# Window-attention scores: the low-part product over all 128 rows instead of over 64

## The chip, the cores and the metric

The kernel runs on one core of a Trainium2 chip. The metric is the device time of one execution in microseconds. Three timed runs of the kernel before gave 893.3, 894.34 and 895.06 us; the median is 894.34 us.

## The reference

One layer of a hybrid decoder over 512 tokens of 1024 channels: a norm, three token mixers side by side (chunked linear attention with 4 heads, a short gated convolution, sliding-window attention), their gated sum, an output projection, a second norm and a gated MLP with 2816 channels and a convolution of width 3. All in float32.

The change lies in the sliding-window attention. It has 8 query heads, 2 key heads and 64 channels per head. The tokens stand in four blocks of 128; a query sees the keys of its own block up to itself and those of the block before that are less than 128 tokens away:

```python
    qb = (q.astype(f32) * hd ** -0.5).reshape(Bsz, Nb, W, Hkv, G, hd)
    kw = windows(k)                       # 256 keys: the block before and its own
    scores = jnp.einsum('bnqhgd,bnkhd->bnhgqk', qb, kw)
    logits = jnp.where(valid[None, :, None, None], scores + alibi, -jnp.inf)
    m = jnp.maximum(logits.max(axis=-1), sink)
    p = jnp.exp(logits - m[..., None])
    denom = p.sum(axis=-1) + jnp.exp(sink - m)
    o = jnp.einsum('bnhgqk,bnkhd->bnqhgd', p, vw) / jnp.moveaxis(denom, 4, 2)[..., None]
```

## The kernel before, in words

Float32 accuracy is made of products in float32r: each factor is split into a high part (its rounding) and a low part (the rest), and a product is high x high + high x low + low x high, without low x low.

The weights come as a stream of blocks of 2048 columns per partition (class W, lines 52 to 101): SyncE loads a block, ScalarE writes its high part (line 91), VectorE its low part (line 92), a block or more ahead of the products that use it. The large products take most of the time: by_channel (line 171; its products all stand on line 177) and by_token (lines 183 to 186). Every 12 products by_channel calls tick, which advances the tasks in the list `side` by one step each. Linear attention and window attention run as such side tasks beside the large products.

The window attention's queries come from four tiles of 128 channels (lines 595 to 602), each of which holds two heads in its lower and upper 64 rows. For each head there is a tile sq with the query's high part in the head's own 64 rows and its low part in the other 64 rows. The keys are stored for either of the 2 key heads as skh (high part) and skl (low part), each of them twice, in the lower and in the upper 64 rows (lines 605 to 609). So a product over all 128 rows of sq and skh gives high x high + low x high in one instruction, and one over the 64 rows that hold the query's high part, with skl, adds high x low.

window(n) handles one block of 128 queries. Its steps, one at each tick: the scores of four heads (scores(0)), then those of the other four (scores(1)) while the first are evicted by ScalarE (line 655), masked (line 656), given their bias and reduced to a maximum by VectorE (line 660); the exponentials on ScalarE (line 680); the division on VectorE (line 686); eight transposes on TensorE (line 693); their eviction with a mask on VectorE (line 698); the products with the values on TensorE (line 706), and the split of the result (lines 709 and 710). A window starts five steps behind the one before. The order in which the instructions of an engine are put down is not that of the Python text alone: a planner with a simulated timeline (line 988) may move them.

The stationary operand of each score product is the block of 128 queries, and 256 keys of skh or skl move past it. Each product has its own weight load (PEld in the profile), also where two in a row have the same stationary operand. One call of scores gives eight products into two banks of PSUM; four windows with two calls each give 64.

Of the kernel before, what the change touches and what calls it, by code (L numbers as in the profile page):

```python
# [23 lines left out]
EPS = 1e-6  # L24
TAU = 16.0
NCONST = 6 * P
NSLOT = 45  # scratch tiles of [128, 512] up to the output projection
HEAD_STEPS = 3  # steps from the start of one linear-attention head to that of the next
LAG_STEPS = 5  # steps that a head's products wait for their factors
WINDOW_STEPS = 5  # steps from one window's start to the next one's  # L30

GQ, GK, GV, GR, GA = 0, 512, 1024, 1536, 2048
CX, CB, CC = 2064, 2576, 3088
# [4 lines left out]
def trunk(ctx, tc, x, g_mix, w_in, w_alpha, b_alpha, norm_g, conv_w, sinks, w_gla, w_conv, w_swa,  # L38
# [11 lines left out]
        return ps.tile([P, 512], F32, tag="b", name="bank")  # L50

    class W:
        """A stream of weight blocks of 2048 columns per partition, each split exactly into two
        float32r parts. While the products of block i run, block i + 1 is split, in pieces, and
        block i + 2 is loaded."""

        def __init__(self):
            self.todo, self.raw, self.done, self.pieces = [], [], [], []
# [45 lines left out]
    at = {}  # L104
    side = []

    def tick():
        """One step of whatever runs beside the large products."""
        w.piece()
        for task in list(side):  # L110
            if next(task, side) is side:
                side.remove(task)
# [78 lines left out]
        nc.vector.tensor_sub(out=lo, in0=src, in1=hi.bitcast(F32))  # L191

    def rstd_of(ss, n, tag, log=False):
        """(ss / n + EPS) ** -0.5, refined by one Newton step."""
        shape = list(ss.shape)
        v = small.tile(shape, F32, tag=tag + "v", name="v")
        r = small.tile(shape, F32, tag=tag + "r", name="r")
        t = small.tile(shape, F32, tag=tag + "t", name="t")
        nc.vector.tensor_scalar(out=v, in0=ss, scalar1=1.0 / n, scalar2=EPS, op0=ALU.mult, op1=ALU.add)
        if log:  # L200
            nc.scalar.activation(out=t, in_=v, func=AF.Ln)
            nc.scalar.activation(out=r, in_=t, func=AF.Exp, scale=-0.5)
        else:
            nc.scalar.activation(out=t, in_=v, func=AF.Sqrt)
            nc.vector.reciprocal(out=r, in_=t)
        u = small.tile(shape, F32, tag=tag + "u", name="u")
        nc.vector.tensor_mul(out=u, in0=r, in1=r)
        nc.vector.tensor_mul(out=u, in0=u, in1=v)
        nc.vector.tensor_scalar(out=u, in0=u, scalar1=-0.5, scalar2=1.5, op0=ALU.mult, op1=ALU.add)
        nc.vector.tensor_mul(out=r, in0=r, in1=u)  # L210
        return r

    def rstd_1(ss, e, n, tag, log=False):
        """(ss / n + e[0]) ** -0.5 for one column, refined by one Newton step; e[1] is -e[0] / 2."""
        v = small.tile([P, 1], F32, tag=tag + "v", name="v")
        r = small.tile([P, 1], F32, tag=tag + "r", name="r")
        t = small.tile([P, 1], F32, tag=tag + "t", name="t")
        if log:
            nc.scalar.activation(out=t, in_=ss, func=AF.Ln, scale=1.0 / n, bias=e[0])
            rstd_1.last = nc.scalar.activation(out=r, in_=t, func=AF.Exp, scale=-0.5)  # L220
        else:
            nc.scalar.activation(out=t, in_=ss, func=AF.Sqrt, scale=1.0 / n, bias=e[0])
            nc.vector.reciprocal(out=r, in_=t)
        nc.vector.tensor_scalar(out=v, in0=ss, scalar1=-0.5 / n, scalar2=e[1], op0=ALU.mult, op1=ALU.add)
        nc.vector.tensor_scalar(out=v, in0=v, scalar1=r, scalar2=r, op0=ALU.mult, op1=ALU.mult)
        nc.vector.tensor_scalar(out=r, in0=v, scalar1=1.5, scalar2=r, op0=ALU.add, op1=ALU.mult)
        return r

    def rstd_part(ss, n, tag, engine=nc.vector):
        """The first part of a sum of squares, for rstd_1 of the rest."""  # L230
        e = small.tile([P, 2], F32, tag=tag + "e", name="e")
        engine.tensor_scalar(out=e[:, 0:1], in0=ss, scalar1=1.0 / n, scalar2=EPS, op0=ALU.mult, op1=ALU.add)
        engine.tensor_scalar_mul(e[:, 1:2], e[:, 0:1], -0.5)
        return e[:, 0:1], e[:, 1:2]

    # ---- the input and its norm
    zero = pc.tile([P, 256], F32, name="zero")
    nc.vector.memset(zero, 0.0)
    idle = bank()

    def warm(n):
        """Products of zeros, to hold the tensor engine's clock up until the input is there."""
        for _ in range(n):
            mm(idle[:, 0:256], zero[:, 0:P], zero, start=True, stop=True)

# [78 lines left out]
        return ul[:, k, :]  # L324

    def a_tile(name, j, n=slice(0, S), acc=None):
        """Tile j of the channels of a weight block, by token."""
        if name == "gq0":
            hi, lo = (a.rearrange("p (j k c) -> p j k c", j=2, c=P)[:, j] for a in w.take(at[name]))
        else:  # L330
            hi, lo = (a.rearrange("p (k j c) -> p j k c", j=2, c=P)[:, j] for a in w.take(at[name]))
        acc = acc or bank()
        by_channel(acc, lambda k: hi[:, k], lambda k: lo[:, k], uhk, ulk, n=n)
        return acc

    def b_tiles(name):
        """The four token tiles of 512 channels, each as it is ready."""
        accs = [bank() for _ in range(NT)]
        for i in range(2):
            hi, lo = (a.rearrange("p (k c) -> p k c", c=512) for a in w.take(at[f"{name}{i}"]))  # L340
            for t in range(NT):
                tok = slice(t * P, (t + 1) * P)
                by_token(accs[t], lambda k: uh[:, 4 * i + k, tok], lambda k: ul[:, 4 * i + k, tok],
                         lambda k: hi[:, k, :], lambda k: lo[:, k, :], 4, i == 0, i == 1)
                if i:
                    yield t, accs[t]

    # ---- linear attention: queries, keys and gates
    qs, ks = [None] * GH, [None] * GH

    def got_q(h, acc):
# [78 lines left out]
            la[h] = z  # L430

    def running_sums(y, n):
        """In place: the sums of the first 1, 2, .. n of every n columns."""
        s = 1
        while s < n:
            g = y.rearrange("p (g s) -> p g s", s=2 * s)
            nc.vector.tensor_add(out=g[:, :, 2 * s - 1], in0=g[:, :, 2 * s - 1], in1=g[:, :, s - 1])  # L437
            s *= 2
        s = n // 4
        while s:  # L440
            g = y.rearrange("p (n g s) -> p n g s", s=2 * s, g=n // (2 * s))
            nc.vector.tensor_add(out=g[:, :, 1:, s - 1], in0=g[:, :, 1:, s - 1], in1=g[:, :, :-1, 2 * s - 1])
            s //= 2

    # ---- linear attention: the factors of each head
    ATs, qIs, kTs, decs = [None] * GH, [None] * GH, [None] * GH, [None] * GH

    def factors(h):
# [89 lines left out]
        nc.scalar.copy(out=v, in_=acc)  # L538
        vs.append(v)

    # ---- linear attention: states and outputs
    Os = [None] * NT

    def normed(n, O):
# [44 lines left out]

    side.append(states())  # L590

    # ---- window attention
    lower, upper = slice(0, 64), slice(64, 128)
    sqs = []
    for t in range(4):
# [36 lines left out]
    def window(n):  # L632
# [6 lines left out]
        def scores(pr):  # L639
            sps = [bank() for _ in range(2)]  # L640
            for i in range(2):
                for g in range(2):
                    rg = upper if i else lower
                    q = sqs[4 * g + 2 * pr + i]
                    s_ = sps[i][:, 256 * g:256 * g + 256]
                    mm(s_, q[:, c], skh[g][:, kc], start=True, stop=False)  # L646
                    mm(s_, q[rg, c], skl[g][rg, kc], start=False, stop=True)  # L647
            return sps

        def biased(pr, sps):  # L650
            """Each query's last 128 keys: those of its own block up to itself, the others of the block before."""
            for i in range(2):
                s = slot(name="sc")[:, 0:256].rearrange("p (g j) -> p g j", g=2)
                ps2 = sps[i].rearrange("p (g j) -> p g j", g=2)
# [63 lines left out]
    side.append(values())  # L718
    side.append(windows())

    # ---- short convolution
    def conv3(acc, cwj, name):
        """Three causal taps over the tokens, from PSUM or SBUF."""
        y = slot2(name=name)
        nc.scalar.activation(out=y, in_=acc, func=AF.Copy, scale=cw[:, 2, cwj:cwj + 1])  # L725
        nc.vector.scalar_tensor_tensor(out=y[:, 1:], in0=acc[:, :S - 1], scalar=cw[:, 1, cwj:cwj + 1],  # L726
# [24 lines left out]
            och.append(hi)  # L751
            ocl.append(lo)

    # ---- linear attention: output gate
    ogh = [slot(F32R, name="ogh") for _ in range(4)]
    ogl = [slot(F32R, name="ogl") for _ in range(4)]

# [15 lines left out]
    for t, acc in b_tiles("gr"):  # L773
        side.append(gated(t, acc))

    # ---- the gated sum of the branches
    mh, ml = [], []
    for j in range(4):
        gts = []
# [29 lines left out]
    uh = pU.tile([P, KT, S], F32R, name="uh2")  # L809
    ul = pU.tile([P, KT, S], F32R, name="ul2")  # L810

    # ---- output projection, residual, norm
    gf = [slot(name="gf") for _ in range(2)]
    for i in range(2):
        nc.gpsimd.dma_start(out=gf[i], in_=g_ffn[None, 512 * i:512 * i + 512].to_broadcast([P, 512]))
# [47 lines left out]
                elif two:  # L863
                    h_split(t - 2, hn[t - 2])

    # ---- gated MLP with a convolution
    first3 = [("ug0", 0), ("ug0", 1), ("uu0", 0)]
    early = []
    for i, (name, j) in enumerate(first3):
# [19 lines left out]
    xs = [None] * len(DOWN)  # L889

    def split_prods(i):
        """The factors of block i, split a tile at each step."""
        k0, kt = DOWN[i]
        xs[i] = [[], []]
        for k in range(kt):
            for part, name in zip(xs[i], ("xh", "xl")):
                part.append(pF.tile([P, 512], F32R, tag="t", name=name, bufs=22))
            split(xs[i][0][k], xs[i][1][k], prods[k0 + k])
            yield
# [92 lines left out]
```

## Time and profile before

| | |
|---|---|
| median of 3 timed runs | 894.34 us (893.3 to 895.06) |
| span of the profiled execution | 891.6 us |
| median of the timed runs less that span | 2.7 us |
| PE (TensorE products) busy | 879.0 us, 99% |
| PEld (weight loads) busy | 705.9 us, 79% |
| DVE (VectorE) busy | 475.2 us, 53% |
| ACT (ScalarE) busy | 342.8 us, 38% |
| mean granted TensorE clock | 0.996 |

The span is that of one profiled execution, from the first to the last instruction. What lies around it in that execution isn't given by itself; the timed runs stand 2.7 us above the span. Durations of products are pipelined and their ends are modelled, so a product's duration is longer than its distance to the next one. The window scores lie between 147 and 219 us.

### The profile page before, as it was taken

To read this page: it belongs to the slowest core of one execution; us is meant where nothing else is said; L and a number is where in the kernel's file an instruction comes from. 1 tells how busy PE (TensorE), PEld (TensorE's weight loads), DVE (VectorE), ACT (ScalarE), POOL (GpSimd) and SP (SyncE) were. 2 spreads that over 40 slices of the span, in tenths; PEclk is the share of its full clock that TensorE was granted. 3 is DMA by queue.
4 is the path that set the end of the run, shared out by engine and by line. 5 is a ranking of instruction groups with operands and counts; after the bars stand their busy time and mean duration, and the time that the engine had idled before them with its cause. 6 is when DMAs were issued, how large, how long until landed. Compare 5 with 4: busy or idle time off the path is not lost.

```text
span 891.6 us, 10006 instructions
## 1 busy us (share of the span) xinstructions
PE 879.0 (99%) x3976; PEld 705.9 (79%) x3976; DVE 475.2 (53%) x822; ACT 342.8 (38%) x607; POOL 59.1 (7%) x58
## 2 busy tenths in 40 slices
PE   8999999999999999999999999999999999999996
PEld 6887887767678888888888898888888888888885
DVE  5599566765633251526234666555555555743734
ACT  6545543443434132322223444333333333532533
POOL 2027003000000000101010000000000000001100
PEclk9999999999999999999999999999999999999999
DMA  9431331211222333233325134222222223222202
GB/s 278 145 94 48 95 95 48 86 56 48 78 66 71 95 93 115 77 95 96 87 79 165 48 118 139 93 92 93 94 92 93 92 69 113 96 71 95 95 1 94
DMA packets 69862, 82.39 MB, mean 92 GB/s; under 512 B 2875, under 2 KB 58455, under 8 KB 69815
## 3 DMA queue, kind: packets, MB, share of 16 engines
q1 hardware_dynamic: 69511, 80.70, 28.4%
q0 software_dynamic: 304, 1.05, 0.4%
q8 instruction: 31, 0.51, 0.2%
q14 instruction: 16, 0.13, 0.0%
HBM read 79.64 MB, written 2.10 MB: 92 GB/s over the span
## 4 chain that ended last, share of the span: by engine, by line
PE 92%; DVE 4%; ACT 1%; POOL 1%; issue 0%; DMA 0%; ACTq 0%
PE bank L177 64%; PE bank L184 7%; PE bank L183 7%; PE bank L186 7%; PE bank L647 1%; PE bank L706 1%; PE bank L646 1%; DVE wlo L92 1%; POOL d L461 1%; DVE z L437 1%; DVE d L479 0%; PE bank L693 0%; PE bank L566 0%; DMA h<-in_x 0%; ACT xsq L299 0%
## 5 line engine op out<-in xcount | busy, mean ns | idle before, releaser
L177 PE MATMUL bank<-uh,whi 128*128 128x512 f32 (+1 forms) x792 | 302.7, 386 | 1.9 <-ACT uh L315 1.6
L177 PE MATMUL bank<-ul,whi 128*128 128x512 f32 (+1 forms) x792 | 303.1, 386 | 0.2
L92 DVE TENSOR_TENSOR wlo<-raw,whi 128x1024 fp32r<-128x1024 f32 x144 | 176.5, 1259 | 196.1 <-ACT whi L91 113.0
L91 ACT CAST whi<-raw 128x1024 fp32r<-128x1024 f32 x144 | 144.4, 1048 | 174.6 <-PE bank L177 145.8
L177 PE MATMUL bank<-uh,wlo 128*128 128x512 f32 (+1 forms) x792 | 192.8, 384 | 0.0
L177 PEld LDWEIGHTS bank<-uh,whi 128*128 128x128 f32 x792 | 149.4, 189 | 35.5 <-ACT uh L315 2.1
L177 PEld LDWEIGHTS bank<-ul,whi 128*128 128x128 f32 x792 | 149.8, 189 | 33.4 <-issue 0.8
L177 PEld LDWEIGHTS bank<-uh,wlo 128*128 128x128 f32 x792 | 144.0, 188 | 32.3 <-issue 0.8
L184 PE MATMUL bank<-whi,xl 128*128 128x512 f32 x176 | 68.8, 392 | 0.0
L183 PE MATMUL bank<-whi,xh 128*128 128x512 f32 x176 | 67.9, 391 | 0.0
L186 PE MATMUL bank<-wlo,xh 128*128 128x512 f32 x176 | 48.0, 391 | 0.0
L191 DVE TENSOR_TENSOR xl<-p,xh 128x512 fp32r<-128x512 f32 x44 | 30.2, 726 | 26.9 <-ACT xh L190 22.6
L183 PEld LDWEIGHTS bank<-whi,xh 128*128 128x128 f32 x176 | 33.1, 188 | 7.3
L186 PEld LDWEIGHTS bank<-wlo,xh 128*128 128x128 f32 x176 | 33.1, 188 | 7.2
L184 PEld LDWEIGHTS bank<-whi,xl 128*128 128x128 f32 x176 | 33.1, 188 | 7.1
L190 ACT CAST xh<-p 128x512 fp32r<-128x512 f32 x44 | 24.7, 616 | 36.3 <-PE bank L184 36.3
L725 ACT ACTIVATE yg<-bank,cw 128x512 f32<-128x512 f32 x22 | 15.1, 685 | 53.3 <-PE bank L177 53.3
L797 DVE TENSOR_TENSOR g<-bank,g 128x512 f32<-128x512 f32 x24 | 16.5, 689 | 32.0 <-PE bank L177 31.4
L800 POOL TENSOR_TENSOR g<-g 128x512 f32<-128x512 f32 x8 | 13.4, 1673 | 302.7 <-DVE g L797 300.7
L784 ACT ACTIVATE g<-bank 128x512 f32<-128x512 f32 x24 | 14.3, 596 | 48.2 <-PE bank L177 48.1
L907 ACT ACTIVATE yg<-yg 128x512 f32<-128x512 f32 x22 | 13.9, 631 | 47.9 <-DVE yg L728 47.9
L726 DVE SCALAR_TENSOR_TENSOR yu<-bank,cw,yu 128x511 f32<-128x511 f32 x22 | 16.4, 747 | 26.4 <-ACT yu L725 26.4
(211 smaller groups left out, 963.1 us busy)
## 6 DMA issues: line engine op xcount, KB each, us to landing
raw<-in_w_in SPq DMA_DIRECT2D x28, 1024.0 KB, 5.2
raw<-in_w_up SPq DMA_DIRECT2D x22, 1024.0 KB, 5.1
raw<-in_w_down SPq DMA_DIRECT2D x10, 1024.0 KB, 5.0
raw<-in_w_o SPq DMA_DIRECT2D x4, 1024.0 KB, 5.0
h<-in_x SPq DMA_DIRECT2D x4, 512.0 KB, 4.8
raw<-in_w_gla_o SPq DMA_DIRECT2D x4, 512.0 KB, 3.4
raw<-in_w_conv_o SPq DMA_DIRECT2D x4, 512.0 KB, 4.6
raw<-in_w_swa_o SPq DMA_DIRECT2D x8, 256.0 KB, 4.1
```

Of the source, the lines that this page charges most:

```text
L91: nc.scalar.copy(out=hi[:, c], in_=raw[:, c])
L92: nc.vector.tensor_sub(out=lo[:, c], in0=raw[:, c], in1=hi[:, c].bitcast(F32))
L177: mm(acc[:, n], a, b[:, n], start=i == 0, stop=i == len(todo) - 1)
L183: mm(acc, xh(k), hi(k), start=start and k == 0, stop=False)
L184: mm(acc, xl(k), hi(k), start=False, stop=False)
L186: mm(acc, xh(k), lo(k), start=False, stop=stop and k == kt - 1)
L190: nc.scalar.copy(out=hi, in_=src)
L191: nc.vector.tensor_sub(out=lo, in0=src, in1=hi.bitcast(F32))
L725: nc.scalar.activation(out=y, in_=acc, func=AF.Copy, scale=cw[:, 2, cwj:cwj + 1])
L726: nc.vector.scalar_tensor_tensor(out=y[:, 1:], in0=acc[:, :S - 1], scalar=cw[:, 1, cwj:cwj + 1], in1=y[:, 1:], op0=ALU.mult, op1=ALU.add)
L784: nc.scalar.activation(out=g, in_=acc, func=AF.Sigmoid)
L797: nc.vector.tensor_mul(out=g, in0=acc, in1=g)
```

## The change

The second product of each score takes all 128 rows of sq and skl. The rows added hold the query's low part and another copy of the key's low part, so the scores get the term low x low as well. The helper variable for the 64 rows goes. Otherwise only comments and docstrings are taken out of the text.

```diff
             for i in range(2):
                 for g in range(2):
-                    rg = upper if i else lower
                     q = sqs[4 * g + 2 * pr + i]
                     s_ = sps[i][:, 256 * g:256 * g + 256]
                     mm(s_, q[:, c], skh[g][:, kc], start=True, stop=False)
-                    mm(s_, q[rg, c], skl[g][rg, kc], start=False, stop=True)
+                    mm(s_, q[:, c], skl[g][:, kc], start=False, stop=True)
             return sps
```

## Rows read from the trace of the kernel before

**Rows 1.** The page: busy us (share of the span) and count; the chain's shares by engine.
```profile
PE 879.0 (99%) x3976; PEld 705.9 (79%) x3976; DVE 475.2 (53%) x822; ACT 342.8 (38%) x607; POOL 59.1 (7%) x58
...
PE 92%; DVE 4%; ACT 1%; POOL 1%; issue 0%; DMA 0%; ACTq 0%
```

**Rows 2.** Windows: stretch, length, busy PE, PEld, DVE, ACT, POOL, clock, DMA share, GB/s.
```profile
145.00:236.00 91.00, 91.00 (x379) 64.91 (x378) 58.67 (x193) 38.24 (x119) 2.55 (x2) 1.00 0.22 70
```

**Rows 3.** Timeline of PE, second score group: start us, us, engine, line, operation, shapes.
```profile
152.38 0.28 PE L646 MATMUL bank<-skh,sq 128*128 128x256 f32 x1
152.59 0.38 PE L647 MATMUL bank<-skl,sq 64*128 64x256 f32 x1
152.90 0.39 PE L646 MATMUL bank<-skh,sq 128*128 128x256 f32 x1
...
154.78 0.50 PE L177 MATMUL bank<-uh,whi 128*128 128x512 f32 x1
155.11 0.40 PE L177 MATMUL bank<-ul,whi 128*128 128x512 f32 x1
155.34 0.40 PE L177 MATMUL bank<-uh,whi 128*128 128x512 f32 x1
```

**Rows 4.** Timeline of the weight loads of the same group.
```profile
152.15 0.19 PEld L646 LDWEIGHTS bank<-skh,sq 128*128 128x128 f32 x1
152.59 0.18 PEld L647 LDWEIGHTS bank<-skl,sq 64*128 64x128 f32 x1 [0.25 <-issue]
152.90 0.19 PEld L646 LDWEIGHTS bank<-skh,sq 128*128 128x128 f32 x1
```

**Rows 5.** Timeline of PE, the value products of window 1.
```profile
204.47 1.94 PE L706 MATMUL bank<-pt,sv 128*64 128x512 f32 x8
206.34 1.20 PE L177 MATMUL bank<-uh,wlo 128*128 128x512 f32 x4
```

**Rows 6.** Timeline of PE, a product of 96 rows and the next one.
```profile
46.24 0.40 PE L422 MATMUL bank<-gl,wa 96*128 96x512 f32 x1
46.48 0.40 PE L177 MATMUL bank<-uh,whi 128*128 128x512 f32 x1
```

**Rows 7.** By tile, skh and skl: count, duration ns min/median/max, first and last start.
```profile
L646 PEld LDWEIGHTS bank<-skh,sq x32: 186/186/192, 146.9 to 218.1; 128*128 128x128 f32 x32
...
L647 PEld LDWEIGHTS bank<-skl,sq x32: 182/183/183, 147.3 to 218.4; 64*128 64x128 f32 x32
...
L609 DVE TENSOR_TENSOR skl<-bank,skh x4: 683/688/695, 135.1 to 138.4; 64x512 fp32r<-64x512 f32 x4
```

**Rows 8.** Timeline of PE, a projection tile made in halves of 256 columns.
```profile
25.86 0.28 PE L177 MATMUL bank<-uh,whi 128*128 128x256 f32 x1
25.98 0.28 PE L177 MATMUL bank<-ul,whi 128*128 128x256 f32 x1
26.10 1.11 PE L177 MATMUL bank<-uh,wlo 128*128 128x256 f32 x8
27.05 0.28 PE L177 MATMUL bank<-ul,whi 128*128 128x256 f32 x1
```

**Rows 9.** Timeline of PE, the transposes of window 0 and a score group behind them.
```profile
171.33 1.03 PE L693 MATMUL bank<-cst,sc 128*128 128x128 f32 x8
172.12 0.36 PE L646 MATMUL bank<-skh,sq 128*128 128x256 f32 x1
```

**Rows 10.** Timeline of PE, the transposes of window 2, around the last score group.
```profile
215.47 0.71 PE L693 MATMUL bank<-cst,sc 128*128 128x128 f32 x5
...
217.78 0.55 PE L693 MATMUL bank<-cst,sc 128*128 128x128 f32 x3
```

**Rows 11.** Timeline of VectorE: the divisions of windows 0 and 2, and a split.
```profile
162.16 1.66 DVE L686 TENSOR_SCALAR sc<-sc,rs 128x128 f32<-128x128 f32 x8
...
207.63 2.36 DVE L92 TENSOR_TENSOR wlo<-raw,whi 128x1024 fp32r<-128x1024 f32 x2 [7.33 <-PE bank L177]
...
211.21 1.06 DVE L686 TENSOR_SCALAR sc<-sc,rs 128x128 f32<-128x128 f32 x5
```

## The prediction

> **What bounds the kernel now.** I read the page's busy table and the head of the chain of waits first: TensorE is busy 99% of the 891.6 us span and carries 92% of the chain [rows 1]. So a change pays by what it does to TensorE's own sequence, or by a wait that it puts there. Next the stage of the change: between 145 and 236 us, where the window scores lie, PE is busy for all 91.00 us at a granted clock of 1.00 (the level of 2.4 GHz), VectorE for 58.67 and ScalarE for 38.24 [rows 2], so no product waits there on another engine. Last the timeline, because a busy share of 99% hides how far apart the products start. That matters here: a row's duration holds a pipeline that overlaps with the next product (a 512-column product lasts 0.40 us, and the next starts 0.23 behind it), so I count from start to start, never by durations.
>
> One score group, lines 646 and 647, has eight products of 256 columns in turn: 128 rows, 64 rows, 128 rows and so on [rows 3]. The first 64-row product starts 0.21 us behind the 128-row one; each later start is 0.31 behind the last ((154.78 - 152.59) / 7), though the neighbours with twice the columns start 0.23 apart. The first 512-column product behind the group also takes 0.33 to its successor (154.78 to 155.11). The weight-load rows say why [rows 4]: line 646's first load starts at 152.15, 0.23 ahead of its product at 152.38, beside the product before it, and is hidden. The later ones start with the record of their own product (152.59 and 152.59, 152.90 and 152.90): they have waited until the product before was through. Such a product's record holds its load, 0.38 us instead of 0.28.
>
> Is it 64 rows that cost this, or going from 128 to 64 and back? Other small products answer. Line 706's products, whose stationary block has 64 columns, run eight in a row in 1.87 us (204.47 to 206.34), 0.23 each, no more than 512 columns of the full array [rows 5]. Line 422's product of 96 rows has 0.24 to the full product behind it, so it loses nothing [rows 6]. Small operands are not slow in themselves; what costs is going over between the full array and a half, and a score group does that eight times, its exit included.
>
> **The change, part by part.** No instruction is added or removed: the 32 products of line 647 stay, with their 32 loads [rows 7], 256 columns each as before; only their contraction goes from 64 to 128 rows, and with it the last half-array products leave the score groups. The data are there: line 609 writes both halves of skl by 139.1 us (last start 138.4 plus 0.69), and the first product that reads them starts at 147.3 [rows 7].
>
> (a) The step of a 256-column product among full ones. The trace has such a stretch: the first projection tile is made in two halves of 256 columns, with a 128x128 load for each product, pairs of products on one stationary block (25.86 and 25.98), and accumulation in one place, all three as the scores will have them. There ten steps take 27.05 - 25.86 = 1.19 us, 0.119 each [rows 8]. The loads hide, though a load of that shape lasts 186 ns [rows 7].
>
> (b) One group, from its first product to the second 512-column product behind it. Before: 155.11 - 152.38 = 2.73 us. After: 8 x 0.119 + 0.233 (a 512-column step, 155.34 - 155.11) = 1.185. The gain is 1.545 us: 0.09 on the first step, 7 x 0.194 on the next ones, 0.10 on the exit.
>
> (c) There are eight groups: four windows with two each, 32 products on either line [rows 7]. Three begin right behind the transposes of line 693 (the one at 172.12, [rows 9]), where the first step is a little longer; I leave that in on both sides. The last group is broken by three transposes [rows 10], but the change of shape is still there eight times (64 rows to a transpose counts as one). So 8 x 1.545 = 12.4 us.
>
> (d) Load length: a full load lasts 186 ns against 183 [rows 7]. Hidden it costs nothing; with the cover gone, 32 x 3 ns = 0.1 us.
>
> (e) What is late next. TensorE will reach everything behind a group 1.55 us sooner. Its products in the stage that need other engines are the transposes of line 693 (behind the last multiplication of line 686) and the value products of line 706 (behind line 698). The tightest that I found is window 2: line 686 ends at 211.21 + 1.06 = 212.27 [rows 11], the transposes start at 215.47 [rows 10], a margin of 3.2 us. One group lies between the event that set VectorE going (the split of line 92 at 207.63, released by TensorE) and those transposes, so 1.6 us are left. Window 0 has 171.33 - 163.82 = 7.5 [rows 9, 11] and loses one group too. So no stall in the forecast. VectorE's 58.67 us fit into 91.00 - 12.4 = 78.6 us with a share of 0.75. The weight stream takes 0.22 of the DMA engines in the stage [rows 2] and would take 0.25.
>
> (f) Behind the stage nothing depends on when it ended: the rest is the same row of full products, and the gain is carried to the end.
>
> Sum: the profiled span goes from 891.6 to 879.2 us. The median of the timed runs, 894.34, stands 2.7 us above that span (what lies around it); I keep these: 894.34 - 12.4 = 881.9 us.
>
> Bounds of (a), the only new step. From below, transposes with 128 columns start 0.099 apart (171.33 to 172.12 for eight, [rows 9]); a product of twice the columns can't be counted faster, and 64 x 0.02 = 1.3 us more gain gives 880.6. From above, the step stays as it is now and only (d) is added: 894.4. I take 0.119, since that row is the same kind of product in every respect that the trace shows.
>
> A rule that speaks against this: the Trainium skill, "TensorE: Matmul & The Clock Gate", section "The mechanism", says that a weight load overlaps products in flight only when the row groups differ. By it full products could never hide their loads from one another, the change would leave a group's loads exposed, and the time would be that of the first rival. The step in (a) disagrees with it here.
>
> **Rivals.**
> 1. The step stays; the change doesn't do what it says. The exposed load would come from something that the change keeps, such as the swap of the moving operand (skh, then skl) on one stationary block, or loads that can't pass a product on the same rows. Then 894.34 + 0.1 = 894.4. For it: line 646's products are full, and their loads are exposed too. Against it: (a) has both properties and steps at 0.119, and 96 rows lose nothing. 4%.
> 2. TensorE gets ahead of the softmax. The gain is there, but transposes or value products wait, because ScalarE and VectorE work through their steps in a fixed order and a margin of 1.6 us is thin. If the four windows, with 3.1 us of gain each, give back up to half, the time is 882 to 888, say 885. For it: window 2's margin. Against it: PE never waits in the stage today, and window 0 keeps 5.9 us. 11%.
> 3. Slower: the order is written by a planner (line 988), and in the last group it has already put transposes between scores. Priced anew, it could put a window's transposes directly behind its second score group. From that group's end (154.78) to the end of line 686 (162.16 + 1.66 = 163.82) window 0 needs 9.0 us of ScalarE and VectorE [rows 3, 11]; with nothing else in TensorE's queue, four windows would stand 36 us: 894.34 - 12.4 + 36 = 918. It turns the sign from 12.4 / 4 = 3.1 us per window on. Against it: 256 columns stay 256 columns, and 16.5 us of products lie between these points today (154.78 to 171.33). 2%.
>
> **How the numbers follow.** The forecast has 83%; its own range is 880.6 to 883.4 (the bound of (a), and a stall of as much as the tightest margin). With rival 2 the range goes to 886.5; runs of the kernel before spread from 893.3 to 895.1, so I begin at 880.0. About 0.2% (1.8 us) is what a measurement can tell from no change. Faster by more than that: forecast and rival 2, 94%. Within: rival 1, 4%. Slower: 2%.
>
> **What would show it.** Step (a): in the timeline of the changed kernel, starts 0.12 apart in lines 646 and 647, records of 0.28 us, and loads that start with the product before theirs; rival 1 has 0.31 there. Step (b): 1.2 us from a group's first product to the second 512-column one behind it. Step (e): no wait of TensorE on line 686 or 698, and PE busy throughout a stage that is 12 us shorter; rival 2 shows such waits, rival 3 large ones with line 693 close behind line 647. Step (f): from the stage to the end, the same duration as before. The prediction is wrong if the stage shrinks by less than 8 us, or if it shrinks by 12 and the rest grows.

## The result and the profile after

The changed kernel takes 881.05 us (median of 4 runs, 880.52 to 881.93) against 894.0 us of the kernel before (4 runs): a ratio of 0.9857, 95% interval 0.9843 to 0.9871. Forecast were 881.9 us in a range of 880.0 to 886.5. The profiled span is 879.3 us where the sum gave 879.2.

The page's first lines, as [rows 1] showed them for before:

```profile
PE 866.5 (99%) x3976; PEld 701.9 (80%) x3976; DVE 474.8 (54%) x822; ACT 342.5 (39%) x607; POOL 59.0 (7%) x58
...
PE 92%; DVE 4%; ACT 1%; POOL 1%; DMA 1%; issue 0%; SPq 0%; ACTq 0%
```

The counts are the same, PE has lost 12.5 us, and its share and its part of the chain stand where they stood. A kernel that is bound by TensorE at 99% can still have 12 us of air in it, if that air lies inside the records.

The second score group on PE's timeline answers to [rows 3] (lines 646 and 647 of before are 645 and 646 now):

```profile
150.93 0.28 PE L645 MATMUL bank<-skh,sq 128*128 128x256 f32 x1
151.05 0.28 PE L646 MATMUL bank<-skl,sq 128*128 128x256 f32 x1
151.17 0.28 PE L645 MATMUL bank<-skh,sq 128*128 128x256 f32 x1
...
151.88 0.40 PE L177 MATMUL bank<-uh,whi 128*128 128x512 f32 x1
152.11 0.39 PE L177 MATMUL bank<-ul,whi 128*128 128x512 f32 x1
```

From its first product to the second 512-column one the group takes 152.11 - 150.93 = 1.18 us, where it took 2.73. The weight loads of the same group, against [rows 4]:

```profile
150.94 0.19 PEld L646 LDWEIGHTS bank<-skl,sq 128*128 128x128 f32 x1
151.05 0.19 PEld L645 LDWEIGHTS bank<-skh,sq 128*128 128x128 f32 x1
151.17 0.19 PEld L646 LDWEIGHTS bank<-skl,sq 128*128 128x128 f32 x1
```

Line 646's load now starts at 150.94, with the product before its own (150.93), and its own product follows at 151.05. It is hidden, and the record of its product holds 0.28 us instead of 0.38.

### The profile page after: what moved, and what is told of

It reads as the page before. It is cut to its first block, busy times and chain, and to the rows that moved or that the text cites. A ratio compares the mean times of both kernels' runs of the same rounds, so it can differ in the third digit from the quotient of the medians.

```text
span 879.3 us, 10006 instructions
## 1 busy us (share of the span) xinstructions
PE 866.5 (99%) x3976; PEld 701.9 (80%) x3976; DVE 474.8 (54%) x822; ACT 342.5 (39%) x607; POOL 59.0 (7%) x58
## 4 chain that ended last, share of the span: by engine, by line
PE 92%; DVE 4%; ACT 1%; POOL 1%; DMA 1%; issue 0%; SPq 0%; ACTq 0%
PE bank L177 65%; PE bank L183 7%; PE bank L184 7%; PE bank L186 7%; PE bank L705 1%; DVE wlo L92 1%; DMA h<-in_x 1%; POOL d L461 1%; DVE z L437 1%; PE bank L645 0%; PE bank L646 0%; DVE d L479 0%; PE bank L566 0%; PE bank L692 0%; DVE E L478 0%
```

## The experiments

The kernels were timed in three sets: the changed kernel; e1, e2, e6 and v1 on one chip; e3, e4 and e5 on another. The kernel before was timed in each set and took 894.0, 892.81 and 893.54 us. I compare each kernel with the kernel before of its own set, and kernels of one set with each other. Line numbers in the fences are those of the kernel named.

**e1 and e2: the half products together.** Theory A is that of the prediction: what costs is going over between the full array and a half. The main rival is that a 64-row product is slow in itself. Both kernels undo the change and only reorder a group: four full products, then four half ones. They differ in the order of these four.

```diff
+            for i in range(2):
+                for g in range(2):
+                    mm(sps[i][:, 256 * g:256 * g + 256], sqs[4 * g + 2 * pr + i][:, c], skh[g][:, kc],
+                       start=g == 0, stop=False)
+            for i, g in ((0, 0), (0, 1), (1, 0), (1, 1)):   # e2: (0, 0), (1, 0), (0, 1), (1, 1)
+                rg = upper if i else lower
+                mm(sps[i][:, 256 * g:256 * g + 256], sqs[4 * g + 2 * pr + i][rg, c], skl[g][rg, kc],
+                   start=False, stop=g == 1)
```

> The kernel before, with 64-row second products, but each score group puts its four 128-row products first and its four 64-row ones behind them (lower, lower, upper, upper half). Theory A (each going over between the full array and a half costs 0.19 us, the 64-row product itself nothing): two changes of shape in a group instead of eight, so 8 x 6 x 0.194 = 9.3 us less than before: 884.7, and starts 0.12 apart inside the 64-row run. Rival B (each 64-row product costs some 0.39 us more, whatever stands beside it): no change, 894. Rival C (a load can't pass a product on the same rows of a half): 128-row steps 0.12, 64-row steps still 0.31, 8 x 4 x 0.194 = 6.2 us less: 887.8.

> As e1, but the four 64-row products of a group alternate between lower and upper half. Theory A: 884.7 if they run one after another; if a lower and an upper one run side by side, a pair takes 0.12 instead of 0.24, 8 x 2 x 0.12 = 1.9 us less: 882.8. Rival B (the 64-row product itself is slow): 894.

Measured: e1 881.92 us against 892.81 (ratio 0.9885, 0.987 to 0.9899), e2 882.69 (0.9891, 0.9877 to 0.9906). So 32 half products on 64 rows stay, and 10 to 11 of the 13 us are won by their order alone: the product itself is not slow, rivals B and C are out. Against the kernel before of their set e1 gains 10.9 us and e2 10.1, where theory A gave 9.3 without pairs and 11.2 with them. So the times alone don't tell whether half products run in pairs; the rows do. The PE timeline of e1, in the second group:

```profile
152.51 0.63 PE L643 MATMUL bank<-skh,sq 128*128 128x256 f32 x4
153.08 0.50 PE L647 MATMUL bank<-skl,sq 64*128 64x256 f32 x4
153.51 0.50 PE L177 MATMUL bank<-uh,whi 128*128 128x512 f32 x1
153.84 0.39 PE L177 MATMUL bank<-ul,whi 128*128 128x512 f32 x1
```

The same in e2:

```profile
150.99 0.63 PE L643 MATMUL bank<-skh,sq 128*128 128x256 f32 x4
151.55 0.51 PE L647 MATMUL bank<-skl,sq 64*128 64x256 f32 x4
151.99 0.50 PE L177 MATMUL bank<-uh,whi 128*128 128x512 f32 x1
152.32 0.39 PE L177 MATMUL bank<-ul,whi 128*128 128x512 f32 x1
```

The four half products take 0.43 us in e1 and 0.44 in e2, from the first start to that of the full product behind them; the load that the entry leaves uncovered and the way out lie in that. One after another, four steps of 0.119 would be 0.48 without either. They run in pairs; cut to a window that ends at 153.09, e1's timeline has two of them already started:

```profile
153.08 0.39 PE L647 MATMUL bank<-skl,sq 64*128 64x256 f32 x2
```

A pair saves a step, two steps a group. With that theory A gives 8 x 0.119 + 0.233 + 2 x 0.194 - 2 x 0.119 = 1.335 us for a group, and both kernels show 1.33 (153.84 - 152.51, 152.32 - 150.99). Against the 1.18 of the change that is 8 x 0.15 = 1.2 us; e6, which is timed as the changed kernel (below), is 0.9 and 1.6 us faster than they are.

The order in e1's program is lower, lower, upper, upper, and yet its pairs are of one lower and one upper product. The last group shows it, where three transposes part the four half products in the middle. In e1 two lower ones stand ahead of the transposes, in e2 a lower and an upper one:

```profile
208.24 0.50 PE L647 MATMUL bank<-skl,sq 64*128 64x256 f32 x2
208.67 0.55 PE L694 MATMUL bank<-cst,sc 128*128 128x128 f32 x3
...
206.82 0.38 PE L647 MATMUL bank<-skl,sq 64*128 64x256 f32 x2
207.14 0.55 PE L694 MATMUL bank<-cst,sc 128*128 128x128 f32 x3
```

Two lower products take 0.43 us by themselves (208.24 to 208.67), as long as all four of an unbroken group; a lower and an upper one take 0.32. So in e1's unbroken groups the first upper product starts beside the first lower one, ahead of the second lower one, which stands before it in the program.

**e6: 96 rows.** Where lies the line between a half and the full array?

```diff
-                    mm(s_, q[:, c], skl[g][:, kc], start=False, stop=True)
+                    r = slice(0, P if i else 96)
+                    mm(s_, q[r, c], skl[g][r, kc], start=False, stop=True)
```

> The changed kernel, but the 16 second products of even heads run over rows 0 to 95 (part of the low x low term left out), the others over 128. Theory A with the line between a half array and more than a half: 96 rows are no change of shape, time as the changed kernel, 881. Rival (any product with fewer than 128 rows exposes the loads on both sides): half of the gain lost, 887.

Measured: 881.06 us against 892.81 (0.9872, 0.9857 to 0.9886), a span of 878.9 us where the changed kernel has 879.3: no cost. A group starts its products with 96 rows as close as those with 128:

```profile
150.59 0.28 PE L647 MATMUL bank<-skl,sq 96*128 96x256 f32 x1
150.71 0.28 PE L645 MATMUL bank<-skh,sq 128*128 128x256 f32 x1
150.83 0.28 PE L647 MATMUL bank<-skl,sq 96*128 96x256 f32 x1
150.95 0.28 PE L645 MATMUL bank<-skh,sq 128*128 128x256 f32 x1
```

From the first score to the product behind the last value product e6 takes 87.5 us, as the changed kernel does (87.42, below). So it isn't "fewer rows than 128" that exposes a load. The line lies between 64 and 96 rows; no run has a number between.

**e4 and e5: a lone product far from the attention.** To take the disputed cost out of the window stage, one product of zeros goes into each of 47 tiles and half tiles of the MLP's gate and up projections.

```diff
             mm(acc[:, n], a, b[:, n], start=i == 0, stop=i == len(todo) - 1)
+            if extra and i == 5:    # e5: slice(0, P) in the place of lower
+                mm(acc[:, 0:256], nil[lower, 0:P], nil[lower, :], start=False, stop=False)
```

> The changed kernel with 47 extra products of zeros, 64 rows by 256 columns, one in the middle of each tile (or half tile) of the up projection, far from the window attention, accumulated in place so that the result stays. Theory A: each costs a step of 0.119 and two changes of shape of 0.194: 47 x 0.507 = 23.8 us over the changed kernel, 905. Rival (the loss in the window stage was special to its softmax, its tiles or its place): 47 x 0.119 = 5.6 us, 887.

> As e4 with the extra products over 128 rows. Theory A: 47 x 0.119 = 5.6 us over the changed kernel, 887; by e4 less e5 a lone half product costs 0.39 us through its two changes of shape. Rival (any odd product in the stream breaks the hiding of loads): the same time as e4.

(Other than expected, neither kernel keeps the layer's result. In the three tiles that are made in halves, the extra product of the second half goes into the first half, which is finished by then; that this is the reason is not shown. The two serve for their times alone.) Measured: e4 904.49 us, e5 885.83, against 893.54 (ratios 1.0124, 1.0109 to 1.0139, and 0.9915, 0.9898 to 0.9931). The planner's order is the same in both, so the difference is the rows alone: 18.66 us, 0.397 for each product, where theory A has 2 x 0.194 = 0.388. The rival that made the loss special to the window stage is out, and so is the one that any odd product breaks the stream. e4's timeline shows where the 0.39 lie:

```profile
503.44 0.28 PE L179 MATMUL bank<-uh,whi 128*128 128x256 f32 x1
503.56 0.28 PE L179 MATMUL bank<-ul,whi 128*128 128x256 f32 x1
503.77 0.38 PE L181 MATMUL bank<-nil 64*128 64x256 f32 x1
504.08 0.39 PE L179 MATMUL bank<-uh,whi 128*128 128x256 f32 x1
504.31 0.28 PE L179 MATMUL bank<-ul,whi 128*128 128x256 f32 x1
```

The same place in e5:

```profile
504.20 0.28 PE L179 MATMUL bank<-uh,whi 128*128 128x256 f32 x1
504.32 0.28 PE L179 MATMUL bank<-ul,whi 128*128 128x256 f32 x1
504.43 0.28 PE L181 MATMUL bank<-nil 128*128 128x256 f32 x1
504.55 0.28 PE L179 MATMUL bank<-uh,whi 128*128 128x256 f32 x1
```

In e5 all steps are 0.11 to 0.12. In e4 the step into the half product is 0.21 (503.56 to 503.77), 0.09 too long; the next, 0.31, is 0.19 too long; the one behind that, 0.23, is 0.11 too long: 0.39 together. Each change has two parts: the next start comes 0.09 later than among full products, and then a load stands uncovered (0.10, the 0.38 against 0.28 of the records).

**e3: without the second product.**

```diff
-                    mm(s_, q[:, c], skh[g][:, kc], start=True, stop=False)
-                    mm(s_, q[:, c], skl[g][:, kc], start=False, stop=True)
+                    mm(s_, q[:, c], skh[g][:, kc], start=True, stop=True)
```

> The changed kernel without the second product of each score (high x low and low x low of the window scores are left out), so 32 products of 256 columns fewer. Theory A (a full product among full ones costs its step alone): 32 x 0.119 = 3.8 us less than the changed kernel, some 877. Rival (the second products are hidden behind something else in the stage, such as the softmax): 881, no change against the changed kernel.

Measured: 878.88 us against 893.54 (0.9838, 0.9824 to 0.9853). Against the changed kernel's ratio that is 0.0019 less, 1.7 us, and against e6's 0.0034, 3.0 us; expected were 3.8, a miss in size. The first of these differences lies within overlapping intervals, so the rival (no change) is excluded by the rows and not by the times. The groups did shrink as expected: four products take 150.81 - 150.34 = 0.47 us to the first full one, half of the changed kernel's 0.95 (151.88 - 150.93). The rest went elsewhere. With fewer products the planner has set other instructions differently, window 1's value products among them:

```profile
192.75 1.08 PE L704 MATMUL bank<-pt,sv 128*64 128x512 f32 x4
193.76 0.50 PE L177 MATMUL bank<-uh,wlo 128*128 128x512 f32 x1
194.19 1.07 PE L704 MATMUL bank<-pt,sv 128*64 128x512 f32 x2
195.19 0.50 PE L177 MATMUL bank<-uh,wlo 128*128 128x512 f32 x1
195.62 1.07 PE L704 MATMUL bank<-pt,sv 128*64 128x512 f32 x2
196.62 0.50 PE L177 MATMUL bank<-uh,whi 128*128 128x512 f32 x1
```

They stand in three pieces, where the changed kernel has the one run of [rows 5] with 1.87 us. From 192.75 to 196.62, less the two full products between (0.233 each), they take 3.40 us: 1.53 more. Window 2 has the same pattern and the same loss (209.78 to 213.88, less three full products). Window 3 stands in three pieces instead of four and wins 1.2 (3.41 us against 4.60, counted in the same way). So 3.8 - 3.06 + 1.2 = 1.9 us are left, between the two measured values. This is counted from the traces; no run puts the order back alone. TensorE's products stand in one and the same order, tile by tile, in the traces of the kernel before, the changed kernel and e6; here, with a changed number of products, they don't.

**v1: value products together.** The same theory on another pair of lines, found in the trace: in windows 0 and 3 the value products stand apart between full ones. One more step lets all their factors be ready.

```diff
         yield
+        yield
         ops = bank()
         for kt in kts:
             for g in range(2):
```

> The changed kernel with one more step between the eviction of the probabilities and the value products (line 705 of the changed kernel), so that a window's value products stand together instead of one by one between full products (windows 0 and 3). Theory A, applied to the 64-column products: alone each takes 1.00 us and 0.10 on the exit; together window 1's four take 1.87. Window 3 goes from 4 x 1.10 to 1.97, window 0 from 2.2 to 1.1: 3.5 us less than the changed kernel, 877.5. Rival (the extra step moves the end of the windows and puts a wait on the gated sum, or the isolated products were no loss): 881 or more.

Measured: 877.74 us against 892.81 (0.9834, 0.9818 to 0.9851); that is 3.3 us less than e6 on the same chip, where 3.5 were expected, and each run is faster than each of e6's (877.18 to 878.01 us against 880.65 to 881.22). The changed kernel's window 3:

```profile
229.33 1.07 PE L705 MATMUL bank<-pt,sv 128*64 128x512 f32 x2
230.33 0.50 PE L183 MATMUL bank<-whi,uh 128*128 128x512 f32 x1
230.76 1.07 PE L705 MATMUL bank<-pt,sv 128*64 128x512 f32 x2
```

v1's window 0 and window 3:

```profile
176.76 1.08 PE L706 MATMUL bank<-pt,sv 128*64 128x512 f32 x4
177.77 0.50 PE L177 MATMUL bank<-uh,whi 128*128 128x512 f32 x1
...
230.37 1.94 PE L706 MATMUL bank<-pt,sv 128*64 128x512 f32 x8
232.24 0.50 PE L183 MATMUL bank<-whi,uh 128*128 128x512 f32 x1
232.58 0.39 PE L184 MATMUL bank<-whi,ul 128*128 128x512 f32 x1
```

Each value product leaves two records (14 products in the program, 28 records); its factors are float32, not float32r. Two products, four records, take 1.01 us together, and one alone, two records, takes 1.00. So here the gain has two parts: fewer changes of shape, and products of the two column halves that run side by side, which one alone can't. How much each part gives is not separated. The way out costs as much as behind the scores: 0.34 us from 232.24 to 232.58, where 512-column products stand 0.233 apart. PE waits for no other engine in that stage.

## Why the prediction was right

Step (a), the 0.119: the changed group starts its products 0.12 apart. Neither bound was met, the 0.099 below or the 0.31 above; the row of the same kind of product was the one to take.

Step (b): 1.18 us for a group where 1.185 were worked out.

Step (c), the sum, from the first score to the full product behind the last value product, in the kernel before and then in the changed one:

```profile
147.08 0.28 PE L646 MATMUL bank<-skh,sq 128*128 128x256 f32 x1
...
246.92 0.50 PE L184 MATMUL bank<-whi,ul 128*128 128x512 f32 x1
```

```profile
147.21 0.28 PE L645 MATMUL bank<-skh,sq 128*128 128x256 f32 x1
...
234.63 0.50 PE L184 MATMUL bank<-whi,ul 128*128 128x512 f32 x1
```

It was 246.92 - 147.08 = 99.84 us and is 234.63 - 147.21 = 87.42, 12.42 less against the sum's 12.4. The group that is broken by transposes kept its place in the changed kernel.

Step (d) played no part: the loads grew from 183 to 189 ns (median) and are hidden.

Step (e): the tightest margin was to shrink from 3.2 to 1.6 us. VectorE's timeline in window 2 of the changed kernel:

```profile
198.38 2.36 DVE L92 TENSOR_TENSOR wlo<-raw,whi 128x1024 fp32r<-128x1024 f32 x2 [4.63 <-PE bank L177]
...
201.96 1.06 DVE L685 TENSOR_SCALAR sc<-sc,rs 128x128 f32<-128x128 f32 x5
```

and PE's:

```profile
204.66 0.71 PE L692 MATMUL bank<-cst,sc 128*128 128x128 f32 x5
```

The divisions end at 203.02, 1.64 us ahead of the transposes. No wait of TensorE on another engine has come into the stage, and PE is busy in all of it:

```profile
145.00:223.50 78.50, 78.50 (x378) 61.02 (x377) 58.46 (x194) 37.88 (x119) 2.63 (x2) 1.00 0.26 81
```

Against [rows 2] the same work of VectorE and ScalarE (58.46 and 37.88 us) lies in 78.5 us instead of 91. Rival 2 did not come about because the margins held, and rival 3 because the planner left the order of TensorE's 3976 products as it was.

Step (f): behind the stage the rest is as long as before. From 223.7 us to its end at 879.3 the changed kernel has 2880 products, in 655.6 us; before, the last 2880 stood in the 655.6 us from 236.0 to 891.6.

The time of 881.9 us stands 0.85 above the measured one although the span is met to 0.1. The term that was too large is the 2.7 us for what lies around the span. The profiled execution of the changed kernel took 881.09 us with a span of 879.3, and every execution whose span is on record stands 1.7 to 1.8 us above its span. The other 0.9 us of the 2.7 will be the distance of the median from the execution that was profiled; for the first set's executions of the kernel before the spans are not on record.

Rival 1 and the rule that stood with it fell at step (a). The Trainium skill, "TensorE: Matmul & The Clock Gate", section "The mechanism", says in its list of what overlaps that a load overlaps running products only when the row group differs; in the changed kernel and in e5 full products hide each other's loads at steps of 0.12, and the measurement decides. (The text above that list also names a background weight buffer as a target for such loads; no run here shows whether that is the way.) The Trainium skill says in "TensorEngine Tiling (Array Packing)", section "Key Properties" under "Tiling Modes", that changing the tiling mode, and not just the tile, drains the engine. e4 agrees with a price on each change of mode, 0.19 us here, and e1 and e2 agree that going over from the lower half to the upper has none. That the delay is a drain no row shows.

Two pieces of the evidence were read wrongly, though the forecast didn't hang on them. I took the eight records of [rows 5] as products of 0.23 us each, no slower than full ones. They are four products with two records each, in float32, and v1 shows that they run side by side in pairs: one takes 1.00 alone, two 1.01. So that row could not show that small operands are not slow in themselves, and that this was right for the 64-row products was luck as far as it rested on this row; it is e1, e2 and e6 that show it. And [rows 4] don't show that a load waits "until the product before was through": by the records, whose ends are modelled, that product still runs for 0.07 us (152.38 + 0.28 against 152.59). What the rows show is that the load starts with its own product.

For e1 I had counted the half products one after another, since its order puts two of the same half next to each other. That they run in pairs all the same is most of the 1.6 us by which e1 gained more than expected.

## What to carry to other kernels

Measure a stream of products from start to start. In these kernels, weight loads that start with their own product, and records 0.1 us longer than their neighbours', marked changes of the array's shape. Where half-array and full-array products alternate, pad the half ones to the full array if their rows can hold something harmless, or put them together; here a lone half product cost 0.39 us beyond its step, and 96 rows cost nothing. A row of the same kind of operation elsewhere in the same trace gave the gain to 0.1 us.

## What the runs showed of the hardware

Half products on different halves of the rows ran in pairs also where the program puts two of the same half first (e1: four in 0.43 us, as in e2, and two lower ones alone in 0.43 too); an upper one then started ahead of a lower one that stands before it in the program. Products on the two column halves do so too: two in 1.01 us, one in 1.00.
